# Sums over partitions: ones as the stationary operand on four column quarters, with 32x32 transposes on VectorE

## The chip, the cores and the metric

The program runs on one core of a Trainium2 chip. A core has TensorE (PE, matrix products, its weight loads listed apart as PEld), VectorE (DVE), ScalarE (ACT), GpSimd (POOL) and SyncE (SP, here the queue that issues most of the loads). Each works through its own list of instructions in order. The matmuls read SBUF and write PSUM. The metric is the time of one execution on the device in microseconds, median of several runs.

## The reference

Two blocks follow one another, on 256 tokens of width 1024, all in float32.

The first block has two layers. In each, a vector `c` is passed through silu and multiplied with `w_mod` (1024 x 6144) to give the modulation, six vectors of 1024 each (shift, scale and gate, twice); a second vector `c_ctx` does the same for 256 context tokens. Then:

```python
h = rms_norm(xl, g_pre_mix[l]) * (1.0 + sc1) + sh1
y, yc = token_mixer(h, hc, ...)
xl = xl + gt1 * rms_norm(y, g_post_mix[l])
h = rms_norm(xl, g_pre_ffn[l]) * (1.0 + sc2) + sh2
xl = xl + gt2 * rms_norm(swiglu(h, ...), g_post_ffn[l])
```

The mixer joins a gated convolution with a layer norm, a differential attention and a pooling branch. The first layer also carries the context tokens, so it works on 512 tokens. The second block has two layers of attention (one with a selection of the best keys, one dilated) with a feed-forward network each, `rms_norm` in front of each part, and a last `rms_norm`. What matters here: each `rms_norm` needs, for each token, the sum of squares over 1024 channels, and the modulation needs sums over 1024 rows of `w_mod`.

## The kernel before

Activations are kept transposed: a tile has 128 channels on the partitions and the tokens along the free dimension, so a vector of 1024 channels is 8 tiles. Each weight is loaded on SP's queue (`raw`, 1 MB at a time), split by ACT (L154) and DVE or POOL (L155) into a high and a low part, and each product is three matmuls (`mm3`, L164 to L166). Helpers put steps into a list with costs, `merge` mixes lists, and `emit` calls them in order. The framework then gives each engine its instructions in the order of priority; a step wrapped in `soon` has a higher one.

Sums over channels are sums over partitions and over tiles. Elementwise work first adds the 8 tiles up (`sq_add`, `y_add`, `mod_v`), and then a matmul with ones sums over the 128 partitions. It stands in three places.

- `col_rms` (L307, read at L309): one matmul for each group of 128 tokens, with the group as weights and one column of ones as the moving operand, so that the sum of token p comes out on partition p. It is called by `conv_ln2` (one with four groups, one with two), by `token_scale` four times and by `final`.
- `y_rms` (L611 and L612, read at L614 and L617): the same for three quantities (squares of y, products of y and x, squares of the gated y), each from two tiles `acc` and `last` that accumulate in PSUM; the second one with twos. `join` calls it five times in full, and `last` once with the first quantity alone. From the sums DVE makes a reciprocal root (`rsqrt`, L269 to L279, a chain of small operations), PE spreads it over the partitions again (`bcast`, L316), and `residual` uses it.
- `flush` in `mod_v` (L484, read at L489): `mod_v` computes the modulation on DVE. `part` multiplies 512 columns of `w_mod` with values of `c`, row tile by row tile, and adds them into one tile for each stream (`c` alone, or `c` and `c_ctx`). `flush` sums each tile over the partitions, four matmuls a stream, and adds the bias `b_mod` into `mc`. It runs for 12 groups with two streams and for 8 with one, between the matmuls of the first layer's mixer and feed-forward network.

`tr_ps` gives one of two PSUM banks, `slot` one of 66 tiles of 128 x 512 in SBUF. `values` (L1261), which is not touched, multiplies attention weights with values for two heads in turns, and writes them to the two halves of 64 partitions.

Of the kernel before, what the change touches and what calls it, by code (L numbers as in the profile page):

```python
# [10 lines left out]
ALU = mybir.AluOpType  # L11
# [3 lines left out]
D = 1024  # L15
T = 256
DFF = 2816
EPS = 1e-6
# [27 lines left out]
class Kern:  # L46
# [254 lines left out]
    def col_rms(self, key, nt, dim):  # L301

        nc = self.nc
        acc = self.v.pop(key)
        ps = self.tr_ps()
        for t in range(nt):
            nc.tensor.matmul(ps[:, t:t + 1], acc[:, 128 * t:128 * t + 128], self.ones[:, 0:1], start=True, stop=True)  # L307
        v = self.small([128, nt])
        nc.vector.tensor_scalar(v, ps[:, :nt], 1.0 / dim, EPS, op0=ALU.mult, op1=ALU.add)  # L309
        return self.rsqrt(v, nt)  # L310

    def bcast(self, r, nt, ps=None, at=0):
# [30 lines left out]
    def setup(self):  # L343
        nc, a = self.nc, self.a
        self.par = {}
        crow = self.slot()
        nc.sync.dma_start(crow[0:8, :128], a["c"][0].rearrange("(k p) -> k p", p=128))
        nc.sync.dma_start(crow[8:16, :128], a["c_ctx"].rearrange("(k p) -> k p", p=128))
        self.ident = self.const([128, 128], "ident")
        nc.sync.dma_start(self.ident, a["k_ident"])  # L350
        self.ones = self.const([128, 128], "ones")
        nc.vector.memset(self.ones, 1.0)
        self.twos = self.const([128, 1], "twos")
        nc.vector.memset(self.twos, 2.0)
        self.xnat = []
        for src in (a["x"][0], a["ctx"][0]):
            for t in range(2):
                for h in range(2):
                    xn = self.slot()
                    self.xnat.append(xn)  # L360
                    nc.scalar.dma_start(xn, src[128 * t:128 * t + 128, 512 * h:512 * h + 512])
        cc = self.const([128, 16], "cc")
        self.transpose_rows(crow[:, :128], 16, cc)
        th = self.small([128, 16])
        nc.scalar.activation(th, cc, AF.Tanh, scale=0.5)
        nc.vector.tensor_scalar(th, th, 1.0, 0.5, op0=ALU.add, op1=ALU.mult)
        nc.vector.tensor_tensor(cc, cc, th, op=ALU.mult)
        self.st1 = self.const([128, 8, 128], "st1", F32R)
        nc.vector.memset(self.st1.bitcast(F32), 0.0)
        v = cc.rearrange("p (s k) -> p k s", s=2)  # L370
        nc.vector.tensor_copy(self.st1[:, :, 0:2], v)
        nc.vector.tensor_tensor(self.st1[:, :, 2:4], v, self.st1[:, :, 0:2], op=ALU.subtract)
        self.cc = cc
        self.mc = [self.const([128, 48, 2], f"mc{l}") for l in range(2)]
        nc.gpsimd.memset(self.mc[1], 0.0)
        self.par_cols(0)
# [85 lines left out]
    def mod_v(self, st, l, groups, streams):  # L462

        nc = self.nc
        accs = {}

        def part(g, h):
            w = self.mraw(l, g, h)
            if h == 0:
                accs[g] = [self.slot() for _ in range(streams)]  # L470
            for k in range(2):
                for i in range(streams):
                    acc = accs[g][i]
                    c = self.cc[:, 8 * i + 2 * h + k:8 * i + 2 * h + k + 1]
                    if h == 0 and k == 0:
                        nc.vector.tensor_scalar(acc, w[:, k], c, None, op0=ALU.mult)
                    else:
                        nc.vector.scalar_tensor_tensor(acc, w[:, k], c, acc, op0=ALU.mult, op1=ALU.add)  # L478

        def flush(g):  # L480
            ps = self.tr_ps()
            for i in range(streams):
                for t in range(4):
                    nc.tensor.matmul(ps[:, 4 * i + t:4 * i + t + 1], accs[g][i][:, 128 * t:128 * t + 128],  # L484
                                     self.ones[:, 0:1], start=True, stop=True)
            del accs[g]
            b = self.par["b_mod", l][:, 4 * g:4 * g + 4]
            for i in range(streams):
                nc.vector.tensor_tensor(self.mc[l][:, 4 * g:4 * g + 4, i], ps[:, 4 * i:4 * i + 4], b, op=ALU.add)  # L489

        for j, g in enumerate(groups):
            for h in range(4):
                st.append(("x", 0.2, lambda g=g, h=h: part(g, h)))
                if h == 2 and j:
                    st.append(("x", 0.05, lambda g=groups[j - 1]: flush(g)))
        st.append(("x", 0.05, lambda: flush(groups[-1])))

    def mod_flush(self, l, g, ps):
# [71 lines left out]
    def y_add(self, m, ps, tok, full):  # L570
# [12 lines left out]
        def put(i, f):  # L583
            if m == 0:
                V["acc", i] = self.slot()
                f(V["acc", i])
                return
            t = self.slot()
            f(t)
            if m == 7:  # L590
                V["last", i] = t
                return
            a = V["acc", i][:, c]
            (nc.vector if m >= 4 else nc.gpsimd).tensor_tensor(a, a, t[:, c], op=ALU.add)  # L594

        put(0, lambda o: nc.scalar.activation(o[:, c], ps[:, c], AF.Square))  # L596
        if full:
            put(1, lambda o: nc.vector.tensor_tensor(o[:, c], z[:, c], x[:, c], op=ALU.mult))
            put(2, lambda o: nc.scalar.activation(o[:, c], z[:, c], AF.Square))

    def y_rms(self, t0, full):

        nc, V = self.nc, self.v
        n = 3 if full else 1
        ps = self.tr_ps()
        for i in range(n):
            for t in range(2):
                c = slice(t0 + 128 * t, t0 + 128 * t + 128)
                o = ps[:, 2 * i + t:2 * i + t + 1]
                w = self.ones[:, 0:1] if i != 1 else self.twos  # L610
                nc.tensor.matmul(o, V["acc", i][:, c], w, start=True, stop=False)  # L611
                nc.tensor.matmul(o, V["last", i][:, c], w, start=False, stop=True)  # L612
        v = self.small([128, 2])
        nc.vector.tensor_scalar(v, ps[:, 0:2], 1.0 / D, EPS, op0=ALU.mult, op1=ALU.add)  # L614
        if full:
            S = self.small([128, 4])
            nc.vector.tensor_copy(S, ps[:, 2:6])  # L617
        r = self.rsqrt(v, 2)
        out = self.bcast(r, 2)
        V["rb"] = out  # L620
        if full:
            for i in range(2):
                self.residual(i, t0)
            b = self.small([128, 2])
            S0 = V["S0"][:, t0 // 128:t0 // 128 + 2]
            for t in range(2):
                c = slice(t, t + 1)
                nc.vector.scalar_tensor_tensor(b[:, c], S[:, 2 + t:3 + t], r[:, c], S[:, c], op0=ALU.mult, op1=ALU.add)
            for t in range(2):
                c = slice(t, t + 1)  # L630
                nc.vector.scalar_tensor_tensor(S0[:, c], b[:, c], r[:, c], S0[:, c], op0=ALU.mult, op1=ALU.add)
            v2 = self.small([128, 2])
            nc.vector.tensor_scalar(v2, S0, 1.0 / D, EPS, op0=ALU.mult, op1=ALU.add)
            self.bcast(self.rsqrt(v2, 2), 2, out, 256)
            for i in range(2, 8):
                self.residual(i, t0)
        V["rb"] = out
# [73 lines left out]

    def rope(self, src, C, S, hi, lo):

        nc = self.nc
        sh = self.slot()[:, :256]

        t = self.slot()[:, :256] if self.phase == 7 else src
        nc.vector.stream_shuffle(sh, src, SWAP16)
        nc.vector.tensor_tensor(t, src, C, op=ALU.mult)
        nc.gpsimd.tensor_tensor(sh, sh, S, op=ALU.mult)  # L720
        if self.phase == 7:
            nc.gpsimd.tensor_tensor(t, t, sh, op=ALU.add)
            nc.scalar.activation(hi, t, AF.Copy)
            nc.gpsimd.tensor_tensor(lo, t, hi, op=ALU.subtract)
        else:
            nc.vector.tensor_tensor(t, t, sh, op=ALU.add)  # L726
            self.split(hi, lo, t)
# [20 lines left out]
    def mixer1(self, l, hs, N, evac_y, mid):  # L748
# [59 lines left out]
        def qk_evac(which):  # L808
            def f(m, ps, which=which):
                p = self.acts(1, 512)[0]  # L810
                hi, lo = p
                sc = 0.125 if which == "q" else 1.0
                C, S = self.ax[which == "q"]
                self.rope(ps[:, :256], C, S, hi[:, :256], lo[:, :256])
                if which == "k" or N == 512:
# [1105 lines left out]
```

## Time and profile before

| | us |
|---|---|
| median of 3 runs | 2303.47 |
| lowest and highest run | 2300.19, 2305.83 |
| the profiled execution | 2300.08 |
| its span, first to last instruction | 2297.9 |
| PE busy | 2172.5 |
| DVE busy | 1622.3 |
| ACT busy | 1083.9 |
| POOL busy | 508.1 |

The profile shows one execution. Busy times overlap between engines. A matmul's record is longer than the time from one matmul to the next, since they are pipelined; what a matmul costs is therefore read from starts. A float32 matmul has two records, one for each pass. Lines such as L484 are lines of the kernel before; `t<-mraw` names what an instruction writes and reads.

### The profile page before, as it was taken

How to read it: one execution, taken by the hardware profiler on the slowest of the kernel's cores; microseconds unless marked ns; L12 is line 12 of the kernel's file. 1: busy time of each engine (PE TensorE's matmuls, PEld its weight loads, DVE VectorE, ACT ScalarE, POOL GpSimd, SP SyncE). 2: the span in 40 equal slices, each digit the busy share in tenths (PEclk: the TensorE clock that was granted, in tenths of full speed). 3: DMA queues.
4: the chain of work that ended last, by engine and by line, in shares of the span. 5: the costliest groups of instructions: out<-in, count | busy, mean ns of one | idle time of the engine just before them, and what ended most of it. 6: DMA issues, size and time to landing. Idle time of an engine off the chain costs nothing.

```text
span 2297.9 us, 37350 instructions
## 1 busy us (share of the span) xinstructions
PE 2172.5 (95%) x14512; PEld 1970.2 (86%) x14512; DVE 1622.3 (71%) x3259; ACT 1083.9 (47%) x2098; POOL 508.1 (22%) x513
## 2 busy tenths in 40 slices
PE   4999999999989999998999899999978999999998
PEld 3777777788888888888888899899976999988998
DVE  5577777858778845567978877765685766676665
ACT  5355565332432222244556555554446544466443
POOL 2354443321230011032333311100243100110000
PEclk8999999999989999998999999999997999999999
DMA  8321112335515656444322455465441555543553
GB/s 277 79 90 56 56 56 74 114 132 180 165 38 159 187 179 199 155 155 128 119 74 86 136 175 178 137 203 183 152 114 53 166 183 181 194 154 105 183 180 120
DMA packets 296626, 319.18 MB, mean 139 GB/s; under 512 B 20545, under 2 KB 264353, under 8 KB 296449
## 3 DMA queue, kind: packets, MB, share of 16 engines
q1 hardware_dynamic: 293072, 311.27, 42.0%
q0 software_dynamic: 2224, 3.43, 0.6%
q8 instruction: 114, 1.87, 0.3%
q10 hardware_dynamic: 1152, 2.10, 0.3%
q14 instruction: 64, 0.52, 0.1%
HBM read 315.72 MB, written 1.05 MB: 138 GB/s over the span
## 4 chain that ended last, share of the span: by engine, by line
PE 71%; DVE 16%; ACT 5%; issue 4%; DMA 2%; POOL 1%; ACTq 0%; DVEq 0%; POOLq 0%; SPq 0%
PE p L164 20%; PE p L165 20%; PE p L166 20%; DVE wlo L155 3%; DVE t L796 1%; PE p L743 1%; DVE t L478 1%; PE p L247 1%; PE p L249 1%; PE tr L883 1%; PE p L248 1%; DVE b L855 1%; PE tr L484 1%; DVE t L258 1%; ACT whi L154 1%
## 5 line engine op out<-in xcount | busy, mean ns | idle before, releaser
L164 PE MATMUL p<-t,whi 128*128 128x256 f32 (+1 forms) x3724 | 1177.1, 320 | 12.6 <-ACT t L560 6.3
L165 PE MATMUL p<-t,whi 128*128 128x256 f32 (+1 forms) x3724 | 1178.3, 317 | 6.3 <-DVE t L659 3.1
L166 PE MATMUL p<-t,wlo 128*128 128x256 f32 (+1 forms) x3724 | 1176.6, 317 | 2.9 <-DVE wlo L155 1.6
L164 PEld LDWEIGHTS p<-t,whi 128*128 128x128 f32 x3724 | 715.8, 194 | 63.8 <-ACT t L560 7.9
L165 PEld LDWEIGHTS p<-t,whi 128*128 128x128 f32 x3724 | 719.8, 193 | 50.4 <-DVE t L659 4.5
L166 PEld LDWEIGHTS p<-t,wlo 128*128 128x128 f32 x3724 | 718.7, 193 | 47.9 <-DVE wlo L155 3.2
L154 ACT ACTIVATE whi<-raw 128x1024 fp32r<-128x1024 f32 (+4 forms) x487 | 491.8, 1020 | 522.9 <-PE p L165 341.5
L155 DVE TENSOR_TENSOR wlo<-raw,whi 128x1024 fp32r<-128x1024 f32 (+4 forms) x443 | 546.1, 1234 | 184.8 <-ACT whi L154 86.5
L155 POOL TENSOR_TENSOR wlo<-raw,whi 128x1024 fp32r<-128x1024 f32 (+2 forms) x44 | 104.2, 2368 | 505.1 <-ACT whi L154 462.7
L478 DVE SCALAR_TENSOR_TENSOR t<-mraw,big,t 128x512 f32<-128x512 f32 x224 | 166.6, 782 | 24.7 <-DMA mraw<-in_w_mod_dram 23.4
L794 POOL TENSOR_TENSOR t<-t,t 128x512 f32<-128x512 f32 (+1 forms) x120 | 137.6, 1147 | 190.0 <-ACT t L793 187.4
L260 ACT ACTIVATE t<-t 128x256 fp32r<-128x256 f32 (+1 forms) x115 | 54.4, 473 | 160.6 <-DVE t L689 118.4
L299 POOL TENSOR_TENSOR t<-t,t 128x256 f32<-128x256 f32 (+1 forms) x27 | 27.1, 1002 | 413.3 <-ACT t L297 412.8
L247 PE MATMUL p<-whi,t 128*128 128x256 f32 x352 | 102.7, 292 | 2.7 <-ACT t L858 2.7
L689 DVE TENSOR_TENSOR t<-t,p 128x256 f32<-128x256 f32 (+1 forms) x91 | 43.2, 474 | 84.0 <-PE p L166 83.9
L796 DVE SCALAR_TENSOR_TENSOR t<-u,big,t 128x512 f32<-128x512 f32 (+1 forms) x120 | 100.7, 839 | 0.8
L743 PE MATMUL p<-t,t 64*128 64x256 f32 (+2 forms) x528 | 77.7, 378 | 23.8 <-DVE t L261 11.7
L249 PE MATMUL p<-whi,t 128*128 128x256 f32 x352 | 100.0, 284 | 0.0
L248 PE MATMUL p<-wlo,t 128*128 128x256 f32 x352 | 99.9, 284 | 0.0
L594 POOL TENSOR_TENSOR t<-t,t 128x256 f32<-128x256 f32 (+1 forms) x36 | 40.5, 1153 | 220.6 <-ACT t L596 217.3
L743 PEld LDWEIGHTS p<-t,t 64*128 64x128 f32 x528 | 50.8, 212 | 44.8 <-issue 18.1
L257 ACT ACTIVATE t<-p 128x256 fp32r<-128x256 f32 x72 | 27.6, 383 | 122.1 <-DVE p L726 98.9
(298 smaller groups left out, 2542.6 us busy)
## 6 DMA issues: line engine op xcount, KB each, us to landing
raw<-in_w_in_dram SPq DMA_DIRECT2D x60, 1024.0 KB, 5.1
raw<-in_l_w_gate_up_dram SPq DMA_DIRECT2D x44, 1024.0 KB, 5.1
raw<-in_w_ffn_in_dram SPq DMA_DIRECT2D x42, 1024.0 KB, 5.2
mraw<-in_w_mod_dram SPq DMA_DIRECT2D x80, 512.0 KB, 4.4
raw<-in_l_w_in_dram SPq DMA_DIRECT2D x15, 1024.0 KB, 5.1
raw<-in_l_w_down_dram SPq DMA_DIRECT2D x16, 896.0 KB, 5.0
t<-in_w_mod_dram SPq DMA_DIRECT2D x32, 256.0 KB, 5.3
raw<-in_w_attn_out_dram SPq DMA_DIRECT2D x8, 1024.0 KB, 5.3
```

What stands on the lines that cost most here:

```text
L154: nc.scalar.activation(p.hi, src, AF.Copy)
L155: eng.tensor_tensor(p.lo, src, p.hi, op=ALU.subtract)
L164: mm(ps, lh, rh, start=first, stop=False)
L165: mm(ps, lh, rl, start=False, stop=False)
L166: mm(ps, ll, rh, start=False, stop=last)
L247: mm(ps[:, :256], lh, p.hi[:, k % 4], start=k == 0, stop=False)
L248: mm(ps[:, :256], lh, p.lo[:, k % 4], start=False, stop=False)
L249: mm(ps[:, :256], ll, p.hi[:, k % 4], start=False, stop=k == 7)
L478: nc.vector.scalar_tensor_tensor(acc, w[:, k], c, acc, op0=ALU.mult, op1=ALU.add)
L743: self.nc.tensor.matmul(out[half], q[i // 2][h, qs], k[i % 2][h, ks], start=i == 0, stop=i == 2)
L794: nc.gpsimd.tensor_tensor(acc, acc, t, op=ALU.add)
L796: i = nc.vector.scalar_tensor_tensor(acc, u, w, acc, op0=ALU.mult, op1=ALU.add)
```

## The change

In all three places the ones become the weights and the data become the moving operand. The weights are 32 columns of ones (or twos), and each matmul writes 32 equal rows to one quarter of the partitions of a PSUM bank: quarter q gets the sums of those tokens (or columns) whose index modulo 128 lies in 32q to 32q + 31. After the four quarters of all quantities VectorE transposes the bank in blocks of 32 x 32 into a `slot` tile. There partition 32q + r holds the sum of token 32q + r of its group, 32 times over, and the first of these is taken. In `flush` the bias is then added for both streams in one operation. `y_rms` reads the sums from that tile, so that its copy from PSUM (L617) falls away. `twos` grows from 1 column to 32.

```diff
--- before.py
+++ after.py
@@ -302,11 +302,9 @@
 
         nc = self.nc
         acc = self.v.pop(key)
-        ps = self.tr_ps()
-        for t in range(nt):
-            nc.tensor.matmul(ps[:, t:t + 1], acc[:, 128 * t:128 * t + 128], self.ones[:, 0:1], start=True, stop=True)
+        S = self.col_sums([[acc[:, :128 * nt]]], nt)
         v = self.small([128, nt])
-        nc.vector.tensor_scalar(v, ps[:, :nt], 1.0 / dim, EPS, op0=ALU.mult, op1=ALU.add)
+        nc.vector.tensor_scalar(v, S[:, 0], 1.0 / dim, EPS, op0=ALU.mult, op1=ALU.add)
         return self.rsqrt(v, nt)
 
     def bcast(self, r, nt, ps=None, at=0):
@@ -350,7 +348,7 @@
         nc.sync.dma_start(self.ident, a["k_ident"])
         self.ones = self.const([128, 128], "ones")
         nc.vector.memset(self.ones, 1.0)
-        self.twos = self.const([128, 1], "twos")
+        self.twos = self.const([128, 32], "twos")
         nc.vector.memset(self.twos, 2.0)
         self.xnat = []
         for src in (a["x"][0], a["ctx"][0]):
@@ -479,14 +477,20 @@
 
         def flush(g):
             ps = self.tr_ps()
+
             for i in range(streams):
-                for t in range(4):
-                    nc.tensor.matmul(ps[:, 4 * i + t:4 * i + t + 1], accs[g][i][:, 128 * t:128 * t + 128],
-                                     self.ones[:, 0:1], start=True, stop=True)
+                a = accs[g][i].rearrange("p (t q r) -> p q t r", q=4, r=32)
+                for q in range(4):
+                    nc.tensor.matmul(ps[32 * q:32 * q + 32, 128 * i:128 * i + 128], self.ones[:, 0:32], a[:, q],
+                                     start=True, stop=True)
             del accs[g]
-            b = self.par["b_mod", l][:, 4 * g:4 * g + 4]
-            for i in range(streams):
-                nc.vector.tensor_tensor(self.mc[l][:, 4 * g:4 * g + 4, i], ps[:, 4 * i:4 * i + 4], b, op=ALU.add)
+            n = 128 * streams
+            t = self.slot()[:, :n]
+            nc.vector.transpose(t, ps[:, :n])
+            nc.vector.tensor_tensor(self.mc[l][:, 4 * g:4 * g + 4, :streams],
+                                    t.rearrange("p (i m c) -> p m i c", i=streams, c=32)[:, :, :, 0],
+                                    self.par["b_mod", l][:, 4 * g:4 * g + 4, None].to_broadcast([128, 4, streams]),
+                                    op=ALU.add)
 
         for j, g in enumerate(groups):
             for h in range(4):
@@ -598,23 +602,31 @@
             put(1, lambda o: nc.vector.tensor_tensor(o[:, c], z[:, c], x[:, c], op=ALU.mult))
             put(2, lambda o: nc.scalar.activation(o[:, c], z[:, c], AF.Square))
 
+    def col_sums(self, terms, nt):
+
+
+        nc = self.nc
+        ps = self.tr_ps()
+        m = 32 * nt
+        for i, xs in enumerate(terms):
+            w = self.twos if i == 1 else self.ones[:, 0:32]
+            for j, x in enumerate(xs):
+                v = x.rearrange("p (t q r) -> p q t r", q=4, r=32)
+                for q in range(4):
+                    nc.tensor.matmul(ps[32 * q:32 * q + 32, m * i:m * i + m], w, v[:, q],
+                                     start=j == 0, stop=j == len(xs) - 1)
+        n = m * len(terms)
+        t = self.slot()[:, :n]
+        nc.vector.transpose(t, ps[:, :n])
+        return t.rearrange("p (i t c) -> p i t c", t=nt, c=32)[:, :, :, 0]
+
     def y_rms(self, t0, full):
 
         nc, V = self.nc, self.v
         n = 3 if full else 1
-        ps = self.tr_ps()
-        for i in range(n):
-            for t in range(2):
-                c = slice(t0 + 128 * t, t0 + 128 * t + 128)
-                o = ps[:, 2 * i + t:2 * i + t + 1]
-                w = self.ones[:, 0:1] if i != 1 else self.twos
-                nc.tensor.matmul(o, V["acc", i][:, c], w, start=True, stop=False)
-                nc.tensor.matmul(o, V["last", i][:, c], w, start=False, stop=True)
+        S = self.col_sums([[V[x, i][:, t0:t0 + 256] for x in ("acc", "last")] for i in range(n)], 2)
         v = self.small([128, 2])
-        nc.vector.tensor_scalar(v, ps[:, 0:2], 1.0 / D, EPS, op0=ALU.mult, op1=ALU.add)
-        if full:
-            S = self.small([128, 4])
-            nc.vector.tensor_copy(S, ps[:, 2:6])
+        nc.vector.tensor_scalar(v, S[:, 0], 1.0 / D, EPS, op0=ALU.mult, op1=ALU.add)
         r = self.rsqrt(v, 2)
         out = self.bcast(r, 2)
         V["rb"] = out
@@ -625,7 +637,7 @@
             S0 = V["S0"][:, t0 // 128:t0 // 128 + 2]
             for t in range(2):
                 c = slice(t, t + 1)
-                nc.vector.scalar_tensor_tensor(b[:, c], S[:, 2 + t:3 + t], r[:, c], S[:, c], op0=ALU.mult, op1=ALU.add)
+                nc.vector.scalar_tensor_tensor(b[:, c], S[:, 2, c], r[:, c], S[:, 1, c], op0=ALU.mult, op1=ALU.add)
             for t in range(2):
                 c = slice(t, t + 1)
                 nc.vector.scalar_tensor_tensor(S0[:, c], b[:, c], r[:, c], S0[:, c], op0=ALU.mult, op1=ALU.add)
```

## Rows read from the trace of the kernel before

**Rows 1.** The page: busy time, share of the span and instructions.

```profile
PE 2172.5 (95%) x14512; PEld 1970.2 (86%) x14512; DVE 1622.3 (71%) x3259; ACT 1083.9 (47%) x2098; POOL 508.1 (22%) x513
```

**Rows 2.** The chain that ended last: shares of the span by line.

```profile
by line: PE p L164 20.4%; PE p L165 20.1%; PE p L166 20.0%; issue 3.7%; DVE wlo L155 2.8%; DVE t L796 1.2%; PE p L743 1.1%; DVE t L478 1.0%; PE p L247 1.0%; PE p L249 1.0%; PE tr L883 1.0%; PE p L248 1.0%; DVE b L855 0.9%; PE tr L484 0.9%; 
```

**Rows 3.** L489 over the span: count, ns min/median/max, first and last start.

```profile
L489 DVE TENSOR_TENSOR big<-tr,big x32: 144/155/165, 474.8 to 1022.9; 128x4 f32<-128x4 f32 x32
```

**Rows 4.** Busy us by stretch (instructions), then granted clock, DMA share, GB/s.

```profile
460.00:620.00 160.00, 159.32 (x786) 134.15 (x785) 118.01 (x160) 55.13 (x76) 35.57 (x20) 0.99 0.52 167
640.00:800.00 160.00, 152.51 (x909) 137.03 (x908) 133.66 (x269) 47.90 (x87) 29.06 (x27) 0.97 0.42 132
800.00:1030.00 230.00, 230.00 (x1104) 193.68 (x1103) 129.77 (x177) 68.75 (x99) 41.89 (x22) 1.00 0.54 173
```

**Rows 5.** Waits: engine, line and releaser: us in total, times, longest.

```profile
PE tr L316 <- DVE c L279: 8.3, 7, 3.9
```

**Rows 6.** Groups by line: shapes, count, busy us, mean ns, idle before and releaser.

```profile
L484 PE MATMUL tr<-big,t 128*128 128x1 f32 x256 | 29.8, 244 | 0.7 <-DVE t L478 0.7
...
L503 DVE STREAM_TRANSPOSE t<-t 32x512 f32<-32x512 f32 x4 | 2.8, 700 | 8.8 <-ACT t L502 8.8
...
L718 DVE STREAM_SHUFFLE t<-p 128x256 f32<-128x256 f32 x56 | 25.0, 446 | 0.0
...
L888 DVE COPY t<-tr 128x128 f32<-128x128 f32 x48 | 13.6, 284 | 21.2 <-PE tr L883 21.1
...
L489 DVE TENSOR_TENSOR big<-tr,big 128x4 f32<-128x4 f32 x32 | 4.3, 156 | 33.2 <-PE tr L484 33.0
```

**Rows 7.** PE in time order around one flush: start, duration, entries.

```profile
472.73 0.39 PE L166 MATMUL p<-t,wlo 128*128 128x512 f32 x1
472.95 0.16 PE L484 MATMUL tr<-big,t 128*128 128x1 f32 x1
...
474.65 0.49 PE L164 MATMUL p<-t,whi 128*128 128x512 f32 x1
474.98 0.40 PE L165 MATMUL p<-t,whi 128*128 128x512 f32 x1
```

**Rows 8.** PE in time order around two calls of `values`.

```profile
2050.37 0.28 PE L166 MATMUL p<-t,wlo 128*128 128x256 f32 x1
2050.58 0.43 PE L1261 MATMUL tr<-t,t 128*64 128x256 f32 x1
2050.84 0.39 PE L1261 MATMUL tr<-t,t 128*64 128x256 f32 x2
...
2086.40 2.17 PE L1261 MATMUL tr<-t,t 128*64 128x256 f32 x24
...
2086.88 0.39 PE L1261 MATMUL tr<-t,t 128*64 128x256 f32 x2
2086.89 0.60 PE L1261 MATMUL tr<-t,t 128*64 128x256 f32 x3
2087.09 0.39 PE L1261 MATMUL tr<-t,t 128*64 128x256 f32 x2
...
2088.29 0.28 PE L1261 MATMUL tr<-t,t 128*64 128x128 f32 x2
2088.50 0.39 PE L166 MATMUL p<-t,wlo 128*128 128x256 f32 x1
2088.72 0.28 PE L164 MATMUL p<-t,whi 128*128 128x256 f32 x1
2088.84 0.28 PE L165 MATMUL p<-t,whi 128*128 128x256 f32 x1
```

**Rows 9.** In time order: the end of the first `y_rms`.

```profile
632.55 0.36 PE L165 MATMUL p<-t,whi 128*128 128x256 f32 x1
...
634.52 0.16 DVE L614 TENSOR_SCALAR c<-tr 128x2 f32<-128x2 f32 x1 [2.76 <-PE tr L612]
634.60 0.15 DVE L617 COPY c<-tr 128x4 f32<-128x4 f32 x1
```

## The prediction

> **What bounds the kernel now.** I read the page's busy times first, then the chain that ended last, then busy time by stretch, then single instructions in order of time around the sums that are changed. The page shows TensorE (PE) busy 95% of the span and VectorE (DVE) 71% [rows 1]. The chain that ended last runs through the split matmuls L164 to L166 for 60% of the span, and the sums of the modulation (L484) stand in it by name with 0.9%, some 20 us [rows 2]. The program makes 20 flushes, six calls of `y_rms` and seven of `col_rms`. The flushes all lie between 472 and 1023 us: their 32 reading additions (two for each of 12 flushes, one for each of 8) start from 474.8 to 1022.9 [rows 3]. In the stretches that hold the flushes PE is busy 159.32 of 160 us, 152.51 of 160 and 230.00 of 230, at a granted clock of 0.97 to 1.00 (the upper level, 2.4 GHz), while DVE has 42, 26 and 100 us to spare [rows 4]. So there one microsecond less of PE work should be one microsecond less of time, and extra DVE work should hide. At the `y_rms` calls it is a chain of waits: sums, then DVE, then the broadcast L316, for which PE stood idle 8.3 us in seven places [rows 5].
>
> **What is removed.** Every sum now is a float32 matmul with the data as weights and one column moving. Each call shows as two entries: L484 has 256 for its 128 calls [rows 6]. A two-stream flush (8 calls, 16 entries) takes PE from 472.95 to 474.65, 1.70 us or some 0.11 an entry, and the second matmul behind it starts 0.33 us after the first, where 0.22 is the step in front of the flush: 1.80 us in all [rows 7]. A one-stream flush is 8 entries of 0.111, so 0.89, and 0.02 behind it (half of 1.80, rounded up): 0.91. There are 12 of the first and 8 of the second.
>
> **What a column part costs.** No quarter occurs before, but `values` (L1261) puts float32 sums on two column halves, with 64-column weights and 256 or 128 moving columns, each call again two entries. In the dense stretch entries start in pairs 0.01 us apart (2086.88 and 2086.89), pair after pair 0.21 us later; 24 entries, 12 of each width, take 2.17 us [rows 8]. So an entry streams 256 columns in 0.214 us and 128 in 0.107, and the second pass of one half runs beside the first pass of the other: serial they would take 12 x 0.321 = 3.85, two at a time 1.93, plus the 0.28 of the last one's end. A quarter's weights are half as wide, its moving columns are 128 in a flush and 64 in the other sums. I take the same order, two at a time: 0.107 us a call of 128 columns, 0.053 a call of 64, plus one such slot for each run of calls.
>
> The change of form has a price. From L166 at 2050.37 to the first L1261 at 2050.58 is 0.21 (step 0.12): +0.09. The next one starts 0.26 later (0.214): +0.05. Behind the last pair, at 2088.29, the next matmul starts 0.21 later (0.107): +0.10, and the one behind it 0.22 later (0.12): +0.10 [rows 8]. That is 0.34 a round trip, against 0.10 now, so +0.24 wherever a sum stands alone between ordinary matmuls.
>
> **Flushes.** Two streams: 9 x 0.107 + 0.34 = 1.30, against 1.80: -0.50, x12 = -6.0. One stream: 5 x 0.107 + 0.34 = 0.88, against 0.91: -0.03, x8 = -0.2. On DVE the two additions of 0.156 become a transpose of 128x256 out of PSUM and one addition. A transpose from PSUM is not in the trace; below, the copy of 128x128 from PSUM takes 0.284, beside it the shuffle of 128x256 from PSUM takes 0.446, above, the transpose of 512 columns in SBUF takes 0.700 [rows 6]. I take 0.45 for 256 columns, 0.30 for 128, 0.37 for 192, 0.25 for 64: some +0.3 a flush, 6 us over all, hidden by DVE's idle time [rows 4]; without that cover it would eat the whole gain. DVE already stands in order behind L484 for 33.0 us [rows 6], with the next `mod_v` accumulations and weight splits queued behind it; that wait stays and gets no longer. The extra slot lives for two DVE operations, and no wait for a free slot shows at L489; its price is taken as nothing.
>
> **y_rms.** A full call had 12 sums, 24 entries, 24 x 0.111 = 2.67 us. It gets 24 calls of 64 columns. The sums do not run in one piece: the first pair runs alone, since its `last` tile is late, and ordinary matmuls such as L165 at 632.55 stand between the rest [rows 9]; over the five full calls I count 16 such pieces, 3.2 each. So 24 x 0.053 + 3.2 x (0.053 + 0.24) = 2.2, -0.45 each, -2.2 for five. The bounds of the 64-column price: 0.053 a call as taken, or 0.107 if entries cannot start more often than every 0.053, the fastest sustained pace in [rows 8] (0.107 a pair); then +0.8 each. The short call (8 calls, two pieces) is +0.1. Then DVE: transpose 0.37, less the copy L617 (0.08 from start to start [rows 9]): +0.3 us in the chain between the last sum and the rsqrt, six times, all taken as exposed: +1.8.
>
> **col_rms.** Six calls with two token groups: 4 x 0.053 + 0.05 - 4 x 0.111 + 0.24 = +0.06, +0.4 in all; the one with four: -0.1. The DVE part, 0.25, is hidden where the following `lin` runs on unscaled activations, and exposed in `final`: +0.25. The wider `twos` adds 31 columns to one memset at the start, 0.04 us by the 0.700 for 512 [rows 6], taken as nothing. No DMA is added, removed or moved, and no instruction changes its engine.
>
> **Sum.** -6.0 - 0.2 - 2.2 + 0.1 + 0.4 - 0.1 + 1.8 + 0.25 = -6.0 us. The profiled execution took 2300.1 us (span 2297.9), which makes 2294.1; the median of the runs, 2303.5, lies 3.4 above it, so I forecast 2297.5 us. The smallest difference I count as one is 0.3%, 6.9 us: the likeliest outcome lies just inside it, to the fast side.
>
> **The rivals.**
> 1. *All four quarters at once.* If both passes of four quarters fill the array together, a set of four calls costs two slots. Flushes: 4 x 0.107 + 0.34 = 0.77 and 0.55, saving 12.4 and 2.9; full `y_rms`: 12 x 0.053 + 0.77 = 1.41, saving 6.3 over five; the rest some -1.2, DVE +2: 2282.7 us. For it: nothing in the program forbids it. Against it: in [rows 8] never more than two entries start together, since a half's second pass waits for its first, and the quarters are issued in that same order. Chance 0.12. The Trainium skill, TensorE: Matmul & The Clock Gate, Measured speedup vs the span model, states that tiles in different column groups start about 4 ns apart and run together; by it this rival would be the outcome, and the trace agrees only as far as two halves.
> 2. *Quarters one after another.* Then a two-stream flush is 16 x 0.107 + 0.34 = 2.05, +0.25 each, a one-stream flush 1.20, +0.29 each, `y_rms` 48 x 0.053 + 0.77 = 3.3, +0.65 each: +3.0 + 2.3 + 3.2, +0.4 for the short call, +1.6 for `col_rms`, DVE +2: +12.5, 2316 us, slower. Against it stand the pairs of [rows 8]. Chance 0.10.
> 3. *Sums scattered among ordinary matmuls.* The order on PE follows priorities, and 632.55 shows a matmul between two sums [rows 9]. Twice as many calls can be cut oftener, and each cut costs a round trip, 0.34. Eight more cuts in each of the five full calls make +13.6, so 2311 us, slower; it decides from 18 more cuts in all. Against it: now there are only 3.2 pieces a call. Chance 0.12.
> 4. *The saved PE time is waited away.* If DVE or the weights are next in line, nothing is left of it and the chains' 2 us may show: 2303 to 2305. For it: DVE is 84% busy between 640 and 800 us; against it: PE stood waiting under 1% in the other two stretches [rows 4]. Chance 0.14.
>
> **How the numbers follow.** The forecast case has 0.52, with an own range of 2291 to 2303 (64-column price, exposed or hidden chains). It is faster by over 0.3% in some 0.23, within it in 0.28, slower in 0.01. Rival 1 adds 0.12 to faster; rival 4 0.13 to same; rivals 2 and 3 give 0.19 to slower and 0.03 to same; 0.01 of rival 4 is slower. Faster 0.35, same 0.44, slower 0.21. For the range I take 2286 to 2313, which leaves out most of rivals 1 and 2.
>
> **What would show it.** In the profile after, a two-stream flush should hold PE about 1.3 us, with starts 0.107 apart in overlapping pairs; starts of four together speak for rival 1, single starts every 0.107 for rival 2, many short runs of sums for rival 3. The transpose of 256 columns should take 0.40 to 0.50 us, and the time from the last sum to L269's successor at a join should grow by 0.3. PE's busy share between 460 and 1030 us should stay near full; idle time there would speak for rival 4. The prediction is wrong if quarters cost differently from halves, or if the order on PE elsewhere is changed by the new durations.

## The result

The changed kernel takes 2288.73 us (median of 5 runs, 2287.25 to 2292.38), the kernel before 2302.21 us in 5 runs on the same chip (2297.32 to 2305.83). The ratio is 0.9946, with a 95% interval of 0.9929 to 0.9964: 0.5% faster, some 12.4 us. The forecast of 2297.5 us had the sign and was too careful: about half of the gain was seen. The profiled execution took 2290.41 us (span 2288.6).

The page's busy times, as in [rows 1]:

```profile
PE 2142.1 (94%) x14664; PEld 1926.7 (84%) x14664; DVE 1633.2 (71%) x3275; ACT 1082.9 (47%) x2096; POOL 505.1 (22%) x513
```

The groups by line and form that take the place of L484, L489 and the sums of `y_rms` in [rows 6]. L616 is the matmul in `col_sums`, L620 its transpose, L489 the transpose in `flush`, L490 the bias:

```profile
L484 PE MATMUL tr<-t,big 128*32 128x128 f32 x256 | 12.0, 290 | 4.7 <-DVE t L476 4.7
...
L616 PE MATMUL tr<-t,big 128*32 128x64 f32 x304 | 8.7, 237 | 4.9 <-DVE t L598 3.3 <-DVE t L299 1.5
...
L489 DVE STREAM_TRANSPOSE t<-tr 128x256 f32<-128x256 f32 x12 | 5.3, 439 | 9.6 <-PE tr L484 9.6
...
L490 DVE TENSOR_TENSOR big<-t,big 128x8 f32<-128x8 f32 x12 | 4.0, 336 | 0.2
```

The flushes hold PE for 12.0 us of busy time where they held it for 29.8. But ahead of them PE now stands idle for 4.7 us, until the last addition of `mod_v` (L476) is done; that was 0.7. The transpose of 256 columns takes 0.44 us.

PE in time order around the first flush with two streams, as in [rows 7]:

```profile
467.13 0.39 PE L166 MATMUL p<-t,wlo 128*128 128x512 f32 x1
467.44 0.65 PE L484 MATMUL tr<-t,big 128*32 128x128 f32 x16
468.02 0.50 PE L164 MATMUL p<-t,whi 128*128 128x512 f32 x1
468.36 0.40 PE L165 MATMUL p<-t,whi 128*128 128x512 f32 x1
```

From L166 to L164 it is 0.89 us, 0.23 of it L166's own step (0.39 long, but the next matmul of that form starts 0.23 later): 0.66. L164 holds its successor up by 0.34 - 0.23 = 0.11. So a flush costs 0.77 us, where it cost 1.80. Looked at in short windows, its 16 entries begin in four groups (a count is that of all entries running together from that start):

```profile
467.46 0.52 PE L484 MATMUL tr<-t,big 128*32 128x128 f32 x9
467.58 0.40 PE L484 MATMUL tr<-t,big 128*32 128x128 f32 x8
467.69 0.40 PE L484 MATMUL tr<-t,big 128*32 128x128 f32 x8
467.80 0.29 PE L484 MATMUL tr<-t,big 128*32 128x128 f32 x4
```

The starts are 0.11 us apart, four entries at each: all four quarters run at once. That is the form and the price of rival 1, which had 0.77.

The stretches of [rows 4], busy us, then granted clock, DMA share, GB/s:

```profile
460.00:620.00 160.00, 156.41 (x823) 128.48 (x822) 122.71 (x165) 56.34 (x83) 38.05 (x25) 0.98 0.50 158
640.00:800.00 160.00, 154.21 (x954) 133.66 (x953) 138.88 (x262) 49.58 (x90) 22.26 (x19) 0.99 0.46 145
800.00:1030.00 230.00, 227.23 (x1204) 188.30 (x1203) 132.74 (x210) 73.83 (x112) 42.51 (x24) 0.99 0.53 172
```

In the first, PE is idle for 3.6 us where it was for 0.7: 3.0 of the 4.7 us of waits ahead of the flushes stand here, the other 1.6 in the second. The 2.8 us in the last are no new wait. They are the pause ahead of the third `y_rms`, which lay behind 1030 us before (10.55 us busy of 13.6 from 1030 to 1043.6) and has moved into the window.

**Where the time is by stage.** The reading of each normalisation's sums (L309 and L614 before, L307 and L629 after) marks the same point of the program in both traces:

| point | before, us | after, us | ahead by |
|---|---|---|---|
| first `y_rms` | 634.5 | 625.6 | 8.9 |
| second | 672.6 | 660.5 | 12.1 |
| third | 1043.6 | 1023.3 | 20.3 |
| fourth | 1081.3 | 1057.1 | 24.2 |
| `conv_ln2`, layer 1 | 1293.1 | 1270.6 | 22.5 |
| fifth, join of layer 1 | 1432.0 | 1418.8 | 13.2 |
| last, one quantity | 1642.2 | 1636.7 | 5.5 |
| first `token_scale` | 1663.9 | 1655.9 | 8.0 |
| `final` | 2290.0 | 2280.7 | 9.3 |

Two things are to be explained: a gain of 24 us by 1081, where TensorE's work alone gives less, and some 14 us given back between 1293 and 1664, in a part of the program that has no flush at all. (At the join of layer 1 and at the last `y_rms` a part of the shift is work of `mem_kv` that the changed kernel does ahead of the reading; at the first `token_scale` that is even again.)

**The loss.** What PE waits for at the broadcasts, as in [rows 5] (L314 is L316 of before):

```profile
PE tr L314 <- DVE c L279: 20.6, 9, 4.3
```

It was 8.3 us in seven places. At the join of layer 1, in time order:

```profile
1408.74 0.54 PE L616 MATMUL tr<-t,big 128*32 128x64 f32 x24
...
1418.38 0.38 DVE L620 STREAM_TRANSPOSE t<-tr 128x192 f32<-128x192 f32 x1
...
1420.10 1.23 DVE L155 TENSOR_TENSOR wlo<-raw,whi 128x1024 fp32r<-128x1024 f32 x1 [1.14 <-ACT whi L154]
1421.24 0.16 DVE L269 TENSOR_SCALAR b<-c 128x2 int32<-128x2 int32 x1
...
1423.02 1.11 PE L314 MATMUL tr<-big,c 128*128 128x128 f32 x4 [4.32 <-DVE c L279]
...
1427.10 1.22 PE L314 MATMUL tr<-big,c 128*128 128x128 f32 x4 [2.97 <-DVE c L279]
```

The last sums end at 1409.28, but DVE transposes them only at 1418.38: in its list, three weight splits and two evacuations of `mem_kv` come first. Then PE stands idle for 4.32 and 2.97 us until `rsqrt` is ready, and in `rsqrt`'s way on DVE stands one more split, L155, which itself waited for ACT. In the kernel before, PE had work here: in its list, 26 matmuls stand between the last sum of this `y_rms` and the first broadcast, none of them of `mem_kv`, the step that prepares the second block's keys and values. In the changed kernel's list there are 77, 48 of them of `mem_kv`, which have run by then. At the last `y_rms` the numbers are 19 and 83, again with 48 of `mem_kv`. At the other joins the lists are alike. So what changed is the order in which the program's own list puts `mem_kv` and the broadcast. The wait is not the whole loss. The 14 us from this broadcast on, before and after:

```profile
1435.13:1449.13 14.00, 10.61 (x73) 9.71 (x73) 13.23 (x41) 4.45 (x8) 7.87 (x11) 0.91 0.25 79
```

```profile
1423.02:1437.02 14.00, 7.93 (x33) 7.15 (x34) 11.57 (x43) 3.20 (x7) 6.20 (x9) 0.51 0.25 79
```

Behind the wait the granted clock is at the lower level nearly throughout (0.51 in e2 and e5 too, which have the same order), and 33 matmul entries get through where 73 did.

**The gain at the joins.** Busy time by stretch between the two `y_rms` of a pair (as in [rows 4]), two stretches before, then the same two after:

```profile
634.50:672.60 38.10, 33.66 (x246) 33.25 (x247) 28.06 (x82) 15.06 (x34) 15.94 (x16) 0.87 0.17 57
1043.60:1081.30 37.70, 34.17 (x238) 33.04 (x238) 29.64 (x86) 16.91 (x30) 11.28 (x9) 0.87 0.35 113
```

```profile
625.60:660.50 34.90, 31.12 (x279) 29.90 (x278) 28.14 (x83) 15.07 (x34) 14.64 (x16) 0.95 0.20 62
1023.30:1057.10 33.80, 29.31 (x265) 27.35 (x264) 29.83 (x85) 15.43 (x28) 11.28 (x9) 0.99 0.41 131
```

Beside 3.2 and 3.9 us less, the granted clock (third number from the end) is different: 0.87 before, 0.95 and 0.99 after. The lower level is 0.5 (1.2 GHz, against 2.4), so a clock of 0.87 over 38.1 us is 9.9 us at the lower level. The prediction had not looked at the clock there.

### The profile page after: what moved, and what is told of

Same layout as the page of the kernel before. It is cut to its first block, busy times and chain, and to the rows that moved or that the text cites. A ratio compares the mean times of both kernels' runs of the same rounds, so it can differ in the third digit from the quotient of the medians.

```text
span 2288.6 us, 37705 instructions
## 1 busy us (share of the span) xinstructions
PE 2142.1 (94%) x14664; PEld 1926.7 (84%) x14664; DVE 1633.2 (71%) x3275; ACT 1082.9 (47%) x2096; POOL 505.1 (22%) x513
## 4 chain that ended last, share of the span: by engine, by line
PE 66%; DVE 19%; ACT 5%; issue 4%; DMA 3%; POOL 2%; ACTq 0%; DVEq 0%; POOLq 0%; SPq 0%
PE p L164 19%; PE p L165 19%; PE p L166 19%; DVE wlo L155 3%; DVE t L476 2%; DVE t L808 1%; PE p L755 1%; PE p L247 1%; PE p L249 1%; PE p L248 1%; DVE b L867 1%; PE tr L895 1%; ACT whi L154 1%; DVE t L258 1%; DMA mraw<-in_w_mod_dram 1%
## 5 line engine op out<-in xcount | busy, mean ns | idle before, releaser
L164 PE MATMUL p<-t,whi 128*128 128x256 f32 (+1 forms) x3724 | 1173.6, 319 | 17.9 <-ACT t L564 7.5
L165 PE MATMUL p<-t,whi 128*128 128x256 f32 (+1 forms) x3724 | 1175.2, 317 | 5.0 <-DVE t L671 2.0
L166 PE MATMUL p<-t,wlo 128*128 128x256 f32 (+1 forms) x3724 | 1171.5, 316 | 2.1 <-POOL wlo L155 1.1
L164 PEld LDWEIGHTS p<-t,whi 128*128 128x128 f32 x3724 | 711.9, 193 | 73.2 <-ACT t L564 8.9
L165 PEld LDWEIGHTS p<-t,whi 128*128 128x128 f32 x3724 | 716.5, 193 | 50.3 <-DVE t L671 2.7
L166 PEld LDWEIGHTS p<-t,wlo 128*128 128x128 f32 x3724 | 716.2, 192 | 46.2 <-DVE wlo L155 1.9
L155 DVE TENSOR_TENSOR wlo<-raw,whi 128x1024 fp32r<-128x1024 f32 (+4 forms) x443 | 542.5, 1226 | 211.0 <-ACT whi L154 100.4
L155 POOL TENSOR_TENSOR wlo<-raw,whi 128x1024 fp32r<-128x1024 f32 (+2 forms) x44 | 101.6, 2309 | 530.7 <-ACT whi L154 464.0
L476 DVE SCALAR_TENSOR_TENSOR t<-mraw,big,t 128x512 f32<-128x512 f32 x224 | 167.9, 786 | 22.8 <-DMA mraw<-in_w_mod_dram 21.4
```

Source lines behind the costliest of these rows:

```text
L155: eng.tensor_tensor(p.lo, src, p.hi, op=ALU.subtract)
L164: mm(ps, lh, rh, start=first, stop=False)
L165: mm(ps, lh, rl, start=False, stop=False)
L166: mm(ps, ll, rh, start=False, stop=last)
```

## The experiments

All are against the kernel before on the same chip, medians of 5 to 12 runs.

| run | us | before | ratio, 95% interval |
|---|---|---|---|
| e1_flush_only | 2290.83 | 2300.16 | 0.9954 [0.9942, 0.9967] |
| e2_norms_only | 2296.55 | 2300.16 | 0.9983 [0.9972, 0.9994] |
| e3_kv_behind | 2274.91 | 2300.16 | 0.9890 [0.9876, 0.9905] |
| e4_kv_behind_before | 2295.81 | 2300.16 | 0.9978 [0.9967, 0.9989] |
| e5_neighbours | 2290.15 | 2299.08 | 0.9957 [0.9942, 0.9973] |
| e6_wide_sums | 2290.62 | 2299.08 | 0.9962 [0.9947, 0.9976] |
| e7_norms_kv_behind | 2282.57 | 2299.08 | 0.9928 [0.9912, 0.9943] |
| e8_flush_and_wide | 2287.31 | 2301.01 | 0.9940 [0.9922, 0.9957] |
| e9_flush_wide_kv | 2278.24 | 2301.01 | 0.9894 [0.9876, 0.9911] |

**Each half alone.** The kernel before with the new `flush`, and the changed kernel with the old one:

```diff
+                for q in range(4):
+                    nc.tensor.matmul(ps[32 * q:32 * q + 32, 128 * i:128 * i + 128], self.ones[:, 0:32], a[:, q],
...
```

```diff
+                for t in range(4):
+                    nc.tensor.matmul(ps[:, 4 * i + t:4 * i + t + 1], accs[g][i][:, 128 * t:128 * t + 128],
+                                     self.ones[:, 0:1], start=True, stop=True)
...
```

> The kernel before with the new `flush` alone; `y_rms` and `col_rms` keep the old sums. Theory (four quarters at once, gain given back by a changed order around `mem_kv`): the order at the `y_rms` calls stays that of before, 12 two-stream flushes save 1.03 us each and 8 one-stream flushes 0.36 each, so some -15 us, about 2287 us, and nothing is given back. Rival (two quarters at a time, as forecast, and the rest of the gain comes from the joins): -6 us, about 2296 us.

> The changed kernel with the old `flush`; `y_rms` and `col_rms` have the new sums. Theory: the first layer's joins gain some 8 to 10 us (shorter sums, and a granted clock near 1.0 in the joins, where the kernel before shows 0.87), but the 48 matmuls of `mem_kv` stand in front of the broadcast at the last two `y_rms` calls, and that costs 10 to 15: between 2300 and 2308 us, no faster than before. Rival (the order is harmless and the loss behind 1081 us has another cause, tied to the flushes or to the loads): the joins' gain stays, 2292 to 2296 us.

The flush alone gives 9.3 us by the medians, between theory and rival. The new sums in the normalisations alone give 3.6 us: neither the loss of the theory nor quite the rival's gain. Together it is the 12 to 13 us of the change. Why the flush gives less than its 15 us of matmul time is taken up with e8.

**mem_kv behind the joins.** In both kernels the two steps of `mem_kv` are moved behind the join that they stood ahead of:

```diff
-            if l == 1:
-                st += self.mem_kv(0)
             st += jm(256 if l == 0 else 0, True)
+            if l == 1:
+                st += self.mem_kv(0)
...
-                st += self.mem_kv(1)
...
                 st.append(H(last))
+                st += self.mem_kv(1)
```

> The changed kernel with one further edit: the steps of `mem_kv` are put into the list behind the join that they stood in front of, at both places. Theory: at the last two `y_rms` calls the broadcast again follows 19 to 28 matmuls behind the sums in place of 77 and 83, the 48 matmuls of `mem_kv` cover the chain, and the 10 to 15 us that were given back stay: about 2276 us, and PE no longer waits 4 us twice for the broadcast's input. Rival: as the changed kernel, 2286 to 2292 us.

> The kernel before with the same move of `mem_kv` behind the joins: the control for the run above. Theory: its order had the broadcast ahead of `mem_kv` already (19 and 26 matmuls behind the sums), so nothing changes: 2299 to 2305 us. Rival (the move is worth 10 us by itself, whatever form the sums have): about 2291 us.

With the move the changed kernel takes 2274.91 us, 13 to 14 us less than without it (by the ratios and by the medians); the kernel before gains 4.4, between its theory and its rival. In the list of e3, 28 and 19 matmuls stand between sums and broadcast where there were 77 and 83, and PE's wait at the broadcasts is back near that of [rows 5]:

```profile
PE tr L314 <- DVE c L279: 10.2, 8, 3.6
```

The stages 1293 to 1432 and 1432 to 1642 of before, 138.9 and 210.2 us long, are 148.2 and 217.9 in the changed kernel and 139.3 and 210.1 in e3. So the theory of the loss stands: 13 to 14 us went to the order of `mem_kv` and the broadcast, or some 9 if the 4.4 that the move gives the kernel before is taken off. The stages speak for the larger number: in e4 these two are 139.3 and 209.6 us, as before, so its 4.4 us come from elsewhere. E3 is the fastest kernel of the study.

**Are neighbours on one quarter slower?** The two loops of the flush exchanged:

```diff
-            for i in range(streams):
-                a = accs[g][i].rearrange("p (t q r) -> p q t r", q=4, r=32)
-                for q in range(4):
+            for q in range(4):
+                for i in range(streams):
+                    a = accs[g][i].rearrange("p (t q r) -> p q t r", q=4, r=32)
```

> The changed kernel with the two loops of the flush exchanged, so that the two calls on one quarter of the array stand one behind the other (128 calls as before, same data, same result). Theory: calls start in order and each waits only for its own quarter, so what makes the flush cheap is that neighbouring calls lie in different quarters. Then a two-stream flush takes some 10 slots of 0.107 us (1.07 us) where the changed kernel shows 4 (0.43 us): +0.64 us for each of 12 flushes, +7.7 us, 2294 to 2298 us; in the trace single entries or pairs, not fours, start together. Rival: each quarter works off a queue of its own, so the order of issue does not matter: four starts of four again, 0.43 us, and 2288 to 2290 us.

The rival is right. PE in time order around the first flush:

```profile
469.02 0.39 PE L166 MATMUL p<-t,wlo 128*128 128x512 f32 x1
469.34 0.66 PE L484 MATMUL tr<-t,big 128*32 128x128 f32 x16
469.93 0.50 PE L164 MATMUL p<-t,whi 128*128 128x512 f32 x1
```

0.91 us from L166 to L164, against 0.89, and the time is that of the change. In which order the quarters are issued makes no difference that these runs can tell.

**The clock by itself.** The kernel before, where in `y_rms` and `col_rms` 64 equal columns move instead of one:

```diff
-        self.twos = self.const([128, 1], "twos")
+        self.twos = self.const([128, 64], "twos")
...
-                o = ps[:, 2 * i + t:2 * i + t + 1]
-                w = self.ones[:, 0:1] if i != 1 else self.twos
+                o = ps[:, 64 * (2 * i + t):64 * (2 * i + t) + 64]
+                w = self.ones[:, 0:64] if i != 1 else self.twos
```

> The kernel before with one thing changed in the sums of the two normalisations: 64 identical columns of ones move instead of one, and the first of the 64 equal results is read. The number of matmuls and their weights stay, and an entry of 0.11 us has room for 64 columns (0.027 to 0.053 us at the upper level). Theory: in the kernel before the granted clock falls to its lower level behind these one-column sums (0.87 over the stages 634.5 to 672.6 and 1043.6 to 1081.3), and part of the gain at the joins of the changed kernel is that its sums move 64 columns. Then these two stages show 0.95 or more here and are 2 to 4 us shorter each, with sums that last as long as before: 2292 to 2298 us in all. Rival: the clock falls for another reason, the stages stay at 0.85 to 0.89 and at 38 us each, and the time is 2300 to 2303 us.

2290.62 us: the theory, with more gained than it asked for, though the second of its two stages got only 1.3 us shorter (36.4 against 37.7). No quarter, no transpose and no matmul fewer, and 8.5 us are gained, two thirds of what the whole change gains. (The order of the list differs a little: 15 to 24 matmuls between sums and broadcast, where it was 16 to 26; what that is worth this run does not separate.) The sums themselves did not get shorter. The group of one of the two lines of sums, first in the kernel before, then here:

```profile
L612 PE MATMUL tr<-big,t 128*128 128x1 f32 x64 | 11.4, 248 | 0.0
```

```profile
L613 PE MATMUL tr<-big,t 128*128 128x64 f32 x64 | 12.1, 270 | 0.0
```

What differs is what comes after them. Two microseconds each around the first `y_rms`, first of before, where the sums start from 631.6 to 634.2, then of e6, where they start from 624.8 to 627.1:

```profile
632.00:634.00 2.00, 2.00 (x20) 2.00 (x20) 0.00 (x0) 0.00 (x0) 0.00 (x0) 1.00 0.00 0
634.00:636.00 2.00, 2.00 (x13) 2.00 (x13) 1.45 (x13) 0.00 (x0) 0.00 (x0) 0.59 0.04 8
636.00:638.00 2.00, 2.00 (x12) 2.00 (x12) 1.10 (x9) 0.28 (x1) 0.00 (x0) 0.56 0.00 0
```

```profile
625.00:627.00 2.00, 2.00 (x19) 2.00 (x20) 0.00 (x0) 0.09 (x1) 0.00 (x0) 1.00 0.00 0
627.00:629.00 2.00, 2.00 (x19) 2.00 (x19) 1.42 (x13) 0.00 (x0) 0.00 (x0) 1.00 0.00 0
```

PE is busy without a gap in both. With one moving column, the clock falls behind the sums and PE gets 12 or 13 matmuls through in 2 us; with 64 it stays at the upper level and gets 19 through. The granted clock of three stretches in every profile: the 4 us behind the sums of the first `conv_ln2`, and the two stretches between `y_rms` calls shown above, each at its own time:

| sums of the normalisations | kernel | behind `conv_ln2` | first pair | second pair |
|---|---|---|---|---|
| 1 column | before | 0.63 | 0.87 | 0.87 |
| 1 column | e1 | 0.60 | 0.87 | 0.91 |
| 1 column | e4 | 0.60 | 0.91 | 0.88 |
| 64 columns, quarters | after | 1.00 | 0.95 | 0.99 |
| 64 columns, quarters | e2 | 1.00 | 0.95 | 1.00 |
| 64 columns, quarters | e3 | 1.00 | 0.90 | 0.99 |
| 64 columns, quarters | e5 | 1.00 | 0.91 | 1.00 |
| 64 columns, quarters | e7 | 1.00 | 0.95 | 1.00 |
| 64 columns | e6 | 1.00 | 0.95 | 0.95 |
| 64 columns | e8 | 1.00 | 0.95 | 0.90 |
| 64 columns | e9 | 1.00 | 0.95 | 1.00 |

(In `conv_ln2` the quarters move 128 columns.) The first column parts without exception. In the others the clock varies from profile to profile, but their mean is 0.89 with one column and 0.96 with 64.

**The sums in the normalisations once the order is mended.** The changed kernel with the old flush and `mem_kv` behind the joins (the diffs of e2 and e3 together):

> The changed kernel with the old flush, and with the two steps of mem_kv moved behind the joins (as in e3_kv_behind). It has the new sums in the normalisations alone, with the order of mem_kv taken out of the comparison. Theory: the two parts of the change add up, and the new sums in the joins are worth some 10 us once mem_kv no longer stands ahead of the broadcast: 2284 to 2288 us. Rival: the new sums in the joins are worth no more than the 3.6 us that e2_norms_only showed, to which moving mem_kv adds the 4.4 us that it gave in e4_kv_behind_before: 2292 to 2296 us.

2282.57 us, just under the theory's range. Against e4, which has the same order and the old sums, the new sums are worth 0.5% (0.9978 to 0.9928), some 11 us. e2 showed only 3.6 because the order took the rest.

**Clock against quarters.** e1's flush with e6's one-pass sums of 64 columns, without and with the move of `mem_kv` (the diffs above put together):

> The kernel before with the new flush on quarters (as in e1_flush_only) and, in the normalisations, the old one-pass form with 64 moving columns (as in e6_wide_sums): no quarter and no transpose in the joins, and mem_kv where it was. Theory: the flush's shorter matmuls and the higher clock at the joins are two separate gains, so they add: 9.3 to 10.6 us of e1_flush_only, or up to 15 us if the clock that e1_flush_only lost between 1024 and 1034 us comes back, and 8.8 us of e6_wide_sums; against a kernel before at 2300 us that is 2276 to 2282 us, less than the change itself. Rival: the joins need the quarters' shorter sums, and what the two gave alone overlaps: 2284 to 2290 us.

> As e8_flush_and_wide, with the two steps of mem_kv behind the joins as in e3_kv_behind, so that against e3_kv_behind (2274.9 us) only the form of the sums in the normalisations differs: one pass with 64 columns and no transpose here, quarters and a transpose there. Theory: nearly all that the normalisations gave is the clock, and the quarters' shorter sums (1.2 us less on TensorE in a full call) are partly paid back by the longer chain on VectorE: 2274 to 2279 us. Rival: the shorter sums count in full, 1.4 us in each of five full calls, less 0.3 in each for the transpose: 2280 to 2284 us.

e9 takes 2278.24 us, within the theory's range, and its interval overlaps that of e3 nearly throughout. So in the normalisations nearly all of the gain comes with the 64 moving columns; that the sums run on quarters adds too little to be told from nothing (3.3 us by the medians, 1 by the ratios). e8, at 2287.31 us, fell to the rival: 13.7 us where the two parts alone gave 9.3 and 8.5. Up to layer 1's join, e8 and e9 give PE the same list. Yet here are 4 and 12 us around the third `y_rms`, e8 and then e9:

```profile
1017.00:1021.00 4.00, 0.78 (x5) 0.58 (x4) 2.47 (x5) 2.37 (x5) 1.54 (x1) 0.80 0.63 197
1021.00:1033.00 12.00, 12.00 (x58) 12.00 (x58) 4.91 (x26) 2.70 (x5) 0.00 (x0) 0.50 0.17 55
```

```profile
1013.50:1017.50 4.00, 0.79 (x7) 0.58 (x6) 2.37 (x4) 2.37 (x5) 1.54 (x1) 1.00 0.64 197
1017.50:1029.50 12.00, 11.99 (x101) 11.76 (x100) 9.23 (x35) 4.58 (x8) 2.38 (x2) 1.00 0.36 115
```

Both stand idle for 3.2 us ahead of the join; every kernel here has a pause in this place, of 2.2 to 3.2 us. Behind it one execution ran for 12 us at the lower level, with 58 entries, and the other at the upper, with 101, which costs the first some 5 us. In this place the clock fell in four of the six profiles with the new flush (e1, e3, e8 and the change), and in one of the five with the old one (e4, for 3 us). So the flush's 15 us of matmul time have two leaks: some 3 to 4 us of waits for `mod_v` ahead of the flushes (3.5 in e1, 4.7 in the change, 0.7 before), which the traces show, and about 5 us of clock in some executions. Together they bring 15 near the 9.3 of e1. One profile a kernel does not tell whether the new flush has a part in the clock's fall, but the granted clock over the whole span is known for every run. Its medians, with the old flush and with the new one: 0.970 (before) and 0.968 (e1), 0.973 (e2) and 0.970 (the change), 0.976 (e7) and 0.973 (e3), 0.975 (e6) and 0.971 (e8). It is lower with the new flush in all four pairs, by 0.002 to 0.004, which over some 2290 us is 5 to 9 us. So the new flush seems to have a part. How it acts stays open, the more so as e9, which has it too, ran at 0.976.

## Why the prediction was right in sign and short in size

**What bounds the kernel: right in the main up to 1080 us.** A microsecond less on PE was taken as a microsecond less of time. Of the flushes' 15 us, 9.3 came through (e1): PE now waits 4 us more for `mod_v`, most of it between 460 and 620 us, which is rival 4 in small, and the clock took the rest as far as is known.

**What a column part costs: the step that failed.** "I take the same order, two at a time" was wrong. The pairs of [rows 8] do not tell one explanation from another: with two halves, at most two can start together whether a second pass waits for a first or not. The prediction read an order of passes into them, and carried it to quarters. Measured, the sixteen entries of a flush take four slots, not nine: 0.77 us where 1.30 was forecast (0.55 where 0.88, with one stream: L166 to L164 is 0.68 us at 856.45). Twelve and eight of these make -15.3 us where -6.2 stands in the sum. The change-of-form price, 0.34 a round trip, was right: 4 x 0.107 + 0.34 is 0.77. The Trainium skill, TensorE: Matmul & The Clock Gate, Measured speedup vs the span model, had this outcome; the trace of the changed kernel agrees with it (the first four entries start within 0.02 us, from 467.44 to 467.46). The chance of 0.12 that the prediction gave rival 1 was too low.

**y_rms: the same step.** The first full call runs in two pieces, not 3.2:

```profile
624.03 0.28 PE L164 MATMUL p<-t,whi 128*128 128x256 f32 x1
624.31 0.78 PE L616 MATMUL tr<-t,big 128*32 128x64 f32 x40
625.02 0.39 PE L165 MATMUL p<-t,whi 128*128 128x256 f32 x1
625.24 0.28 PE L166 MATMUL p<-t,wlo 128*128 128x256 f32 x1
```

From L164 to L165 0.99, less L164's step of 0.12, and 0.10 behind: 0.97 us. A first piece at 621.53 costs 0.53 in the same way. Together 1.5, where 2.2 was forecast and 2.67 stood before.

**DVE: the durations right, the chain short.** 0.44 for the transpose of 256 columns (0.45 taken), 0.38 for 192 (0.37). The chain from the first reading of the sums to L269 grew from 0.19 us (634.52 to 634.71) to 0.63 (625.14 to 625.77), by 0.44 and not by 0.3: 0.8 us over six calls.

**Not in the sum: the clock.** Behind the one-column sums the clock fell, which cost the kernel before some 8.5 us by e6; both forms that move 64 columns give them back. The prediction had a sustained 0.87 in reach, in the stretches between the `y_rms` calls, but read the clock of the long stretches alone.

**Not in the sum: the order.** "If the order on PE elsewhere is changed by the new durations" was named as what could make it wrong, and it happened, though not as rival 3 had it: the sums were not scattered, but `mem_kv` was drawn ahead of two broadcasts. That cost 13 to 14 us by e3, or some 9 with e4's gain taken off.

So the gain of 12.4 us is three terms and not one: the shorter sums, about -21 by rival 1's sum with its chains on DVE taken off; the clock behind the normalisations' sums, about -8.5; and about +17 given back, 13 to 14 of it for the order, the rest the waits ahead of the flushes. e3, where the order is mended, gains 25.3 us, which is the first two less 4. The terms are not strictly separate, since the clock varies from run to run. The sum of the prediction had 6 us. It missed some 15 us of shorter sums and 8.5 of clock on one side and some 17 of loss on the other, which largely cancel: that the time came out inside the stated range of 2286 to 2313 us is in good part luck.

## What to carry to other kernels

Before you price a matmul by its entries, look at the granted clock of the stretch behind it: a dense run of matmuls that move one column each kept TensorE busy here and still left it at half clock for the work that followed. When a change alters durations or adds a step to a chain, compare the order of each engine's list before and after, also where nothing was edited, and put filler work behind the wait that it is to fill. And a pattern seen with two parts leaves open what four will do: give the other outcome its full weight until a run with four has been seen.

## What the runs showed of the hardware

- Float32 matmuls on the four column quarters run at once: 8 calls, 16 entries of 128 columns, go in four starts of four entries, 0.11 us apart. With the order of issue exchanged the flush takes 0.91 us from L166 to L164, against 0.89 (e5).
- A float32 matmul with 128 x 128 weights costs 0.11 us an entry with 1 moving column and with 64 alike: at the first `y_rms` entries in a row start 0.11 us apart in the kernel before and in e6, and 64 entries take 11.4 and 12.1 us of busy time.
- Behind the one-column matmuls of 631.6 to 634.2 us the granted clock fell from 2.4 to 1.2 GHz while PE was busy 2.00 of 2.00 us; in e6, in the same place with 64 columns, it did not. The Trainium skill, TensorE: Matmul & The Clock Gate, HAM oscillation — how this bites in real kernels, names idle gaps as what brings the clock down; here PE is busy for 13.98 of the 14 us ahead, from 620 to 634 us, so that rule alone does not account for it.
- Behind the same pause of 3.2 us, the same list of TensorE instructions ran at the lower level (0.50) in one execution and at the upper (1.00) in another (e8, e9).
